# A list of jobs for the first pieces, rotary scalings spread over steps, and va's accumulators begun in pairs: one change to a two-layer encoder kernel on one core

## The chip, the core and the metric

The kernel runs on one core of a Trainium2 chip. The metric is the device time of one execution in microseconds (us), the median of several executions. A core has TensorE (PE, matrix multiplications; PEld is its loading of the stationary operand), VectorE (DVE), ScalarE (ACT), GpSimd (POOL), and SyncE (SP), which here only issues DMAs. Every engine works through its own instructions strictly in the order in which they were written down; what crosses engines is held together by semaphores.

## What is computed

Two groups of tokens, a prompt of 512 and a sample of 256, go through the same two layers. The reference, cut to what matters here:

```python
def _layer(x, c, norm_g, w_ada, b_ada, w_in, b_gate, rpb, q_norm_g, k_norm_g, w_pa, w_pb, w_out):
    ...
    mod = jax.nn.silu(c) @ w_ada + b_ada
    shift, scale, gate = jnp.split(mod, 3, axis=-1)
    hid = _rms_norm(x, norm_g) * (1.0 + scale[:, None, :]) + shift[:, None, :]
    proj = hid @ w_in
    ...
    qa, ka, va, za, qb, kb, vb, zb, ga, gb = jnp.split(proj, split_at, axis=-1)
    ...
    ya = (oa * jax.nn.silu(za)) @ w_pa
    qh = _axial_rope(_rms_norm(qb.reshape(b, n, GQA_Q_HEADS, HEAD_DIM), q_norm_g))
    kh = _axial_rope(_rms_norm(kb.reshape(b, n, GQA_KV_HEADS, HEAD_DIM), k_norm_g))
    ob = _gqa_attention(qh, kh, vb.reshape(b, n, GQA_KV_HEADS, HEAD_DIM))
    yb = (ob * jax.nn.silu(zb)) @ w_pb
    ...
    merged = g_a * ya + g_b * yb
    return x + gate[:, None, :] * (merged @ w_out)
```

Here `oa` is neighbourhood attention over qa, ka and va, and `g_a`, `g_b` are sigmoids of ga and gb.

After two layers a last RMSNorm gives y. Every large product is made of three matmuls, since each operand is split into a high part (rounded) and a low part (what the rounding left): high by high, high by low, low by high.

## The kernel before

Features lie on the partitions, 8 blocks of 128 (`KC`). `hid[g, k]` is the pair `hh`, `hl` (high and low part of `hid`) of block k for group g, 0 for the prompt and 1 for the sample. Weights come in units of 128 x 1024 (`raw`, 512 KB a DMA, two buffers); `split_one` (L220) makes `whi` on ACT and `low` makes `wlo` on DVE, four buffers each.

**Steps.** Most of the kernel is a row of steps: `step(fn)` (L162) writes down one step's matmuls, then everything that `defer(k, fn)` (L151) put k steps later, then pieces of attention from `slots`. So the code's order is every engine's order, and "deferred by two" means that an evacuation stands behind the matmuls of the next steps in the order of writing.

**The first pieces** (L1043 to L1204) are not steps. `put(t, fn)` notes a piece with a due time t, worked out by hand from constants in `SC` (`T0`, `U`, `ML`, `RL`, `FL`, `HL`, `PL`, `WL`, `TS`, `TR`), and the pieces are then written down in order of t. They are:

- loads in the order x (8 blocks), then four times 8 pieces of `w_ada` (`adaraw`, 256 KB each) and one unit of va's weights, then the sample's x (`x0s`) and the masks;
- for each quarter i and each of scale (`sec` 1) and shift (`sec` 0), two products `q_mul` on PE (tile `adap`), then `c_rows` on ACT, `c_col` on PE (tile `adat`), `c_fin` on DVE; so 16 of `q_mul` and 8 of `c_col`;
- the sum of squares of x: `square` on ACT, adds on POOL and DVE, `sq_sum` on PE (`ssps`), then 1/sqrt by Newton's steps on DVE (`ms`, `ny`, `na`) and its spread to all partitions on PE (`rb`); for the sample later the same;
- per block k: `hid_t` on DVE, `hid_hi` on ACT, `hid_lo` on DVE;
- the 16 pieces of va's prompt part (`va_prompt`, L639: for each k the token tiles 0, 1 and then 2, 3, six matmuls `accw` a piece);
- `warm`: matmuls on a tile of zeros (`junk`) that compute nothing, 10 at the start and one each 0.45 of the due time up to 17.

After them come `va_sample` (8 steps), the four pairs of branch A's q and k, then qb, kvb, za and the rest.

**va's accumulators.** `va_prompt` takes all four accumulators at its first piece: tiles 0 to 2 from `ps_acc` (three PSUM buffers), tile 3 from `ps_o` (one buffer). In layer 1 the three `ps_acc` buffers have just held the output products of layer 0 (`accs`), which `wev` reads (L1578).

**The rotary part.** `q_evac` and `kv_evac` copy a product to `rr` and sum its squares; after `SC["QF"]` = 5 steps `rope_finish` (L1309) runs Newton's steps on DVE and at once multiplies every `rr` by the result, four tiles for the prompt's q, two for the sample's q, three for k. The transposes of q follow in `q_tr_p` (from `SC["QT"]` = 8 steps, every two steps) and `q_tr_s` (from `SC["QST"]` = 9), those of k in `ktr` (8 steps after kvb); their PSUM tiles are `qt` and `kt`, from `ps_t` with two buffers, and DVE and ACT read them into `GQ` and `GK`.

Of the kernel before, what the change touches and what calls it, by code (L numbers as in the profile page):

```python
# [7 lines left out]
F32 = mybir.dt.float32  # L8
# [8 lines left out]
KC = 8  # L17
# [7 lines left out]
SC = dict(  # L25

    LA=7,
    U=0.68,

    ML=0.25,  # L30
    RL=0.75,
    FL=0.6,
    HL=0.5,
    PL=0.3,
    WL=2.6,

    SG="PGPVPGPV",
    TS=1,
    TR=2.5,
    WARM=(10, 1, 17.0, 0.45),  # L40

    PW=("wor01", "wor11", "va3"),

# [2 lines left out]
    RQ=31,  # L46

    QF=5,
    QT=8,
    QTT=2,  # L50
    QS=6,
    QST=9,
    KF=6,
    KT=8,
    SGQ=12,
# [14 lines left out]
def trunk(ctx: ExitStack, tc: tile.TileContext, xT, wst, wad, wsd, vec, gain, trig, mask, eye, rpb, yT):  # L70
# [568 lines left out]
    def va_prompt(l):  # L639

        accs = {}
        v4s.clear()

        def piece(k, h):
            need_unit(("va", l), k // 2)
            if not accs:
                for i in range(4):
                    accs[i] = (ps_acc.tile([128, NP], F32, tag="acc", name="accw") if i < 3
                               else ps_o.tile([128, NP], F32, tag="o", name="accw"))
            for i in (2 * h, 2 * h + 1):  # L650
# [368 lines left out]
    with tc.manual_schedule():  # L1019
# [20 lines left out]
            V.tensor_scalar(out=bhalf[:, 8 * l:8 * l + 8], in0=v_bada(l, 2), scalar1=0.5, scalar2=None, op0=ALU.mult)  # L1040
        V.tensor_scalar(out=bgh, in0=vecs[:, 80:112], scalar1=0.5, scalar2=None, op0=ALU.mult)

        plan = []  # L1043

        def put(t, fn):
            plan.append((t, len(plan), fn))
# [17 lines left out]

        def q_load(sec, k):
            raw = galloc([128, 2, 256], F32, "adaraw")
            S.dma_start(out=raw, in_=wad[sec, k])
            quarter[sec, k] = raw
# [17 lines left out]
        def c_rows(sec, i):  # L1086
            rows_of[sec, i] = ada_rows(acc_of.pop((sec, i)))

        def c_col(sec, i):
            rows_of[sec, i] = ada_col(rows_of[sec, i])  # L1090

        def c_fin(sec, i):
            ada_fin(0, sec, i, rows_of.pop((sec, i)))

        def q_plan(sec, i):
# [20 lines left out]

        def square(k):
            sq[k] = galloc([128, NP], F32, "sq")
            A.activation(out=sq[k], in_=xs[0][k], func=AF.Square)

        def sq_add(k, base, eng):
            eng.tensor_add(out=sq[base], in0=sq[base], in1=sq[k])
            gfree(sq.pop(k))

        def sq_sum(k, first, last):
            if first:
                hcell["ps"] = ps_t.tile([128, 4], F32, tag="t", name="ssps")
            for i in range(4):
                mm(hcell["ps"][:, i:i + 1], sq[k][:, 128 * i:128 * i + 128], ones[:, 0:1],
                   first and i == 0, last and i == 3)  # L1130
            gfree(sq.pop(k))

        def sample_square(k):
            q = galloc([128, NS], F32, "sq")
            A.activation(out=q, in_=xs[1][k], func=AF.Square)
            sq[k] = q

        def sample_add(k):
            if k == 0:
                ssq[1] = sq.pop(0)  # L1140
            else:
                G.tensor_add(out=ssq[1], in0=ssq[1], in1=sq[k])
                gfree(sq.pop(k))

        for k in range(KC):
            kind = SC["SG"][k]
            put(tx[k], lambda k=k: square(k))
            if kind in "VG":
                put(tx[k] + 0.6, lambda k=k, kind=kind: sq_add(k, k - 1, G if kind == "G" else V))
                sq_of = k - 1  # L1150
            else:
                sq_of = k
            if k == KC - 1 or SC["SG"][k + 1] == "P":
                first = sq_of == 0
                t = tx[k] + SC["TS"] + (1.2 if sq_of != k else 0.6)
                put(t, lambda k=sq_of, first=first, last=k == KC - 1: sq_sum(k, first, last))
        tr_ = max(tx[-1] + SC["TR"], t - 0.4)
        for i, sl in enumerate(rms_chain(0, hcell)[1:]):
            put(tr_ + (0.5, 2.7)[i], sl[0])
        tr_ += 3.2  # L1160
        for i in range(4):
            put(tu[i], lambda: split_one(False))
            put(tu[i] + 1.0, low_all)
        va_steps = va_prompt(0)
        th_ = tr_
        tp = 0
        for k in range(KC):
            th_ = max(th_ + 0.7, ta[1, k // 2])
            put(th_, lambda k=k: hid_t(0, 0, k, xs[0][k], hcell["rb"], hst, True))
            t = max(th_ + 0.7, ta[0, k // 2] + 0.6 * (k % 2))  # L1170
            put(t, lambda k=k: hid_hi(0, 0, k, hst))
            put(t + SC["HL"], lambda k=k: hid_lo(0, 0, k, hst))
            tp = max(tp + 2.7, t + SC["HL"] + 0.6 + SC["PL"], tu[k // 2] + SC["WL"])
            for h in range(2):
                put(tp + 1.35 * h, lambda k=k, h=h: step(va_steps[2 * k + h]))


        scell, sst = {}, {}
        for k in range(KC):
            put(txs[k] + 0.1, lambda k=k: sample_square(k))  # L1180
            put(txs[k] + 0.6, lambda k=k: sample_add(k))
        t = txs[-1] + 2.0
        for i, sl in enumerate(rms_chain(1, scell)):
            put(t + (0, 0.4, 2.0)[i], sl[0])
        t += 2.6
        for k in range(KC):
            put(t, lambda k=k: hid_t(0, 1, k, xs[1][k], scell["rb"], sst, True))
            put(t + 0.45, lambda k=k: hid_hi(0, 1, k, sst))
            put(t + 0.9, lambda k=k: hid_lo(0, 1, k, sst))
            t += 0.85  # L1190
        W0, W1, WE, WS = SC["WARM"]
# [6 lines left out]
        put(-100, lambda: warm(W0))  # L1198
        t = T0
        while t < WE:  # L1200
            put(t, lambda: warm(W1))
            t += WS
        for _, _, fn in sorted(plan, key=lambda p: p[:2]):
            fn()  # L1204
        xd = None
        for l in range(DEPTH):

# [101 lines left out]
            def rope_finish(rs, ss):  # L1309

                n, nh = ss.shape[1], ss.shape[2]
                V.tensor_scalar(out=ss, in0=ss, scalar1=1.0 / 64, scalar2=EPS, op0=ALU.mult, op1=ALU.add)
                y = newton(ss.rearrange("p t h -> p (t h)"), n * nh).rearrange("p (t h) -> p t h", h=nh)
                t = 0
                for r in rs:
                    k = r.shape[1]
                    V.tensor_mul(out=r, in0=r, in1=y[:, t:t + k, :].unsqueeze(3).to_broadcast([128, k, nh, 64]))
# [489 lines left out]
```

## Time and profile before

| what | us |
|---|---|
| median of 3 executions | 1269.31 (1268.28 to 1269.43) |
| the profiled execution | 1263.48 |
| its span, first to last instruction | 1261.5 |
| PE busy | 1222.2 |
| DVE busy | 810.8 |
| ACT busy | 580.8 |
| POOL busy | 362.3 |

Times in the trace count from the start of the span. "Busy" on PE counts a matmul as busy while it is in the array, also at the slower clock; a row of the windows view gives that clock as PEclk (1.00 is full speed). In a row of the timeline stand the start, the duration, the engine, line and operation with its tiles and shapes, the count of merged instructions, and in brackets the engine's idle time before it with what ended it. A row of the waits view has the total, the times and the longest.

### The profile page before, as it was taken

Reading aid. Unit: us, or ns where it says so; the run is one execution under the profiler, and the core shown is the slowest. Engines: PE = TensorE matmul, PEld = TensorE weight load, DVE = VectorE, ACT = ScalarE, POOL = GpSimd, SP = SyncE. Lnnn points to the kernel's source line nnn. Section 1 sums busy time; section 2 is a strip of 40 time slices with the busy share of each in tenths; the row PEclk is TensorE's granted clock in tenths of the full one; section 3 lists DMA queues with packets and bytes.
Section 4 is the critical chain, followed back from the end, with each engine's and each line's share of the span. In section 5 each row is a group of like instructions: output and inputs, shape, how many; then the busy total and the mean of one; then the engine's idle time right before and its main releaser. Section 6 shows DMA issues by size and latency. Waiting matters only on the chain.

```text
span 1261.5 us, 19544 instructions
## 1 busy us (share of the span) xinstructions
PE 1222.2 (97%) x7301; PEld 1067.4 (85%) x7301; DVE 810.8 (64%) x1600; ACT 580.8 (46%) x1229; POOL 362.3 (29%) x391
## 2 busy tenths in 40 slices
PE   9899999899999999999989999979999999999997
PEld 6589988888989988887888998878989988878887
DVE  3467876785555457999375678778655545683435
ACT  3347764555555432323153676545555543232323
POOL 0214444443222131111041353644422221221102
PEclk9999998899999999999999999999999999999998
DMA  9333231110111125555452333211111012332334
GB/s 354 126 106 89 81 98 35 36 66 18 51 50 51 44 74 159 177 172 182 147 171 80 93 92 89 59 43 50 35 51 49 19 47 87 125 110 68 112 105 150
DMA packets 48845, 118.28 MB, mean 94 GB/s; under 512 B 5488, under 2 KB 13040, under 8 KB 48752
## 3 DMA queue, kind: packets, MB, share of 16 engines
q1 hardware_dynamic: 48608, 116.98, 29.7%
q8 instruction: 57, 0.93, 0.3%
q14 instruction: 36, 0.29, 0.1%
q10 hardware_dynamic: 144, 0.07, 0.0%
HBM read 110.74 MB, written 6.29 MB: 93 GB/s over the span
## 4 chain that ended last, share of the span: by engine, by line
PE 75%; DVE 14%; ACT 5%; issue 3%; POOL 2%; DMA 0%; DVEq 0%; ACTq 0%; POOLq 0%
PE accp L124 33%; PE accs L124 16%; PE accw L124 8%; PE go L124 3%; PE gtp L944 3%; DVE adaacc L454 3%; PE gsp L124 3%; DVE wlo L237 3%; PE acct L124 2%; ACT p L782 1%; PE sp L124 1%; PE junk L124 1%; PE op L124 1%; DVE ptl L711 1%; ACT whi L231 1%
## 5 line engine op out<-in xcount | busy, mean ns | idle before, releaser
L124 PE MATMUL accp<-hh,whi 128*128 128x512 f32 x512 | 203.0, 396 | 0.0
L124 PE MATMUL accp<-hh,wlo 128*128 128x512 f32 x512 | 200.2, 391 | 2.1 <-DVE wlo L237 2.1
L124 PE MATMUL accp<-hl,whi 128*128 128x512 f32 x512 | 200.1, 391 | 0.0
L237 DVE TENSOR_TENSOR wlo<-raw,whi 128x1024 fp32r<-128x1024 f32 x119 | 157.7, 1326 | 14.9 <-ACT whi L231 14.2
L933 POOL TENSOR_TENSOR gp<-gp,gss 128x512 f32<-128x512 f32 x80 | 89.3, 1118 | 205.8 <-DVE gss L931 179.6
L124 PE MATMUL accs<-hh,whi 128*128 128x256 f32 x512 | 145.9, 285 | 0.0
L124 PE MATMUL accs<-hh,wlo 128*128 128x256 f32 x512 | 144.8, 283 | 0.0
L124 PE MATMUL accs<-hl,whi 128*128 128x256 f32 x512 | 144.7, 283 | 0.0
L231 ACT ACTIVATE whi<-raw 128x1024 fp32r<-128x1024 f32 x124 | 129.9, 1053 | 16.6 <-PE accw L124 8.2
L124 PEld LDWEIGHTS accp<-hh,wlo 128*128 128x128 f32 x512 | 96.1, 188 | 24.4 <-DVE wlo L237 3.8
L124 PEld LDWEIGHTS accp<-hh,whi 128*128 128x128 f32 x512 | 96.3, 188 | 17.6
L124 PEld LDWEIGHTS accp<-hl,whi 128*128 128x128 f32 x512 | 96.4, 188 | 17.4
L124 PEld LDWEIGHTS accs<-hl,whi 128*128 128x128 f32 x512 | 97.9, 191 | 1.4
L124 PEld LDWEIGHTS accs<-hh,whi 128*128 128x128 f32 x512 | 97.8, 191 | 1.3
L124 PEld LDWEIGHTS accs<-hh,wlo 128*128 128x128 f32 x512 | 97.8, 191 | 0.0
L1519 POOL TENSOR_TENSOR th<-th 128x512 f32<-128x512 f32 (+1 forms) x32 | 43.4, 1367 | 171.2 <-DVE th L1512 170.7
L706 ACT ACTIVATE pth<-gtp 128x512 fp32r<-128x512 f32 x80 | 47.8, 597 | 93.0 <-PE go L124 73.3
L454 DVE SCALAR_TENSOR_TENSOR adaacc<-adaraw,csil,adaacc 128x512 f32<-128x512 f32 x112 | 86.6, 828 | 3.9 <-DMA adaraw<-in_wsd 3.9
L711 DVE TENSOR_TENSOR ptl<-gtp,pth 128x512 fp32r<-128x512 f32 x80 | 54.6, 685 | 47.3 <-ACT pth L706 47.3
L124 PE MATMUL accw<-whi,hh 128*128 128x512 f32 x192 | 79.2, 413 | 4.8 <-ACT hh L292 3.0
L124 PE MATMUL accw<-whi,hl 128*128 128x512 f32 x192 | 77.0, 401 | 1.1 <-DVE hl L298 1.1
L124 PE MATMUL accw<-wlo,hh 128*128 128x512 f32 x192 | 76.7, 399 | 0.0
(246 smaller groups left out, 2961.4 us busy)
## 6 DMA issues: line engine op xcount, KB each, us to landing
raw<-in_wst SPq DMA_DIRECT2D x124, 512.0 KB, 3.6
adaraw<-in_wsd SPq DMA_DIRECT2D x64, 256.0 KB, 3.2
adaraw<-in_wad SPq DMA_DIRECT2D x32, 256.0 KB, 6.0
u<-in_rpb SPq DMA_DIRECT2D x16, 354.5 KB, 5.0
u<-in_rpb SPq DMA_DIRECT2D x16, 236.5 KB, 4.3
out_y<-y SPq DMA_DIRECT2D x12, 256.0 KB, 2.5
x<-in_xT SPq DMA_DIRECT2D x8, 256.0 KB, 4.6
res<-in_xT SPq DMA_DIRECT2D x8, 256.0 KB, 3.3
```

Of the source, the lines that this page charges most:

```text
L124: T.matmul(out=out, lhsT=lhsT, rhs=rhs, start=start, stop=stop, skip_group_check=True)
L231: A.activation(out=hi, in_=r, func=AF.Copy)
L237: eng.tensor_sub(out=lo, in0=r, in1=hi.bitcast(F32))
L454: V.scalar_tensor_tensor(out=acc[n, h, g], in0=r, scalar=c, in1=acc[n, h, g], op0=ALU.mult, op1=ALU.add)
L706: A.activation(out=h, in_=t, func=AF.Copy)
L711: V.tensor_sub(out=lo, in0=t, in1=h.bitcast(F32))
L782: A.activation(out=P[:, j, :], in_=P[:, j, :], func=AF.Exp, scale=-1.0, bias=ss[:, j:j + 1], accum_out=ss[:, 2 + j:3 + j])
L933: G.tensor_mul(out=pv_, in0=pv_, in1=ss[:, 4:4 + n].unsqueeze(2).to_broadcast([128, n, w]))
L944: T.transpose(t[:, q, 128 * j:128 * j + 128], src, ident)
L1519: G.tensor_add(out=t[:, sl], in0=t[:, sl], in1=mrg[k][:, sl])
```

## The change

Four things change. The first pieces become jobs: `job(eng, dur, deps, fn, rank, at)` names the engine, a guessed duration, the jobs it depends on and an earliest time, and `run_jobs` takes again and again the job that can start first, with `rank` deciding between equals; loads and `warm` stay at due times. `warm` falls to one each 0.8 up to 16. The sample's x is loaded ahead of the fourth unit of va's weights, the prompt's `ssps` moves from `ps_t` to `ps_acc`. In `va_prompt` each accumulator is taken when it is first written, tile 0 is the one in `ps_o`, and in layer 1 the second and third piece change places. In `rope_finish` only the first two tiles are scaled at once; the third and fourth are deferred by one step. The transposes of q move from 8 to 9 (prompt) and from 9 to 12 steps (sample).

```diff
-    WARM=(10, 1, 17.0, 0.45),
+    WARM=(10, 16.0, 0.8),
...
-    QT=8,
+    QT=9,
...
-    QST=9,
+    QST=12,
...
         def piece(k, h):
             need_unit(("va", l), k // 2)
-            if not accs:
-                for i in range(4):
-                    accs[i] = (ps_acc.tile([128, NP], F32, tag="acc", name="accw") if i < 3
+            for i in (2 * h, 2 * h + 1):
+                if k == 0:
+                    accs[i] = (ps_acc.tile([128, NP], F32, tag="acc", name="accw") if i
                                else ps_o.tile([128, NP], F32, tag="o", name="accw"))
...
-        return [lambda k=k, h=h: piece(k, h) for k in range(KC) for h in range(2)]
+        seq = [(k, h) for k in range(KC) for h in range(2)]
+        if l:
+            seq[1:3] = seq[2:0:-1]
+        return [lambda k=k, h=h: piece(k, h) for k, h in seq]
...
+        def run_jobs(lag=0.12):
+            done, t_free, queue = {}, dict(PE=0.0, ACT=0.0, DVE=0.0, POOL=0.0), list(jobs)
+            out = []
+            while queue:
+                best = None
+                for j in queue:
+                    if any(d not in done for d in j["deps"]):
+                        continue
+                    ready = max([j["at"]] + [done[d] + lag for d in j["deps"]])
+                    start = max(ready, t_free.get(j["eng"], 0.0))
+                    key = (start, j["rank"], j["n"])
+                    if best is None or key < best[0]:
+                        best = key, j
...
         def q_plan(sec, i):
+            deps = [jrow[sec, i - 1]] if i else []
             for k in range(4 * i, 4 * i + 4):
-                t = load(1, lambda k=k: q_load(sec, k)) + SC["ML"]
+                t = load(1, lambda k=k: q_load(sec, k))
                 if k % 2:
-                    put(t, lambda k=k: q_mul(sec, k))
-            t += SC["RL"]
-            put(t, lambda: c_rows(sec, i))
-            put(t + 0.4, lambda: c_col(sec, i))
-            put(t + 0.4 + SC["FL"], lambda: c_fin(sec, i))
+                    m = job("PE", 0.6, deps, lambda k=k: q_mul(sec, k), 0, t)
+                    deps = [m]
+            jrow[sec, i] = job("ACT", 0.4, [m], lambda: c_rows(sec, i), 0)
+            c = job("PE", 0.5, [jrow[sec, i]] + last_fin, lambda: c_col(sec, i), 0)
+            jfin[sec, i] = job("DVE", 0.4, [c], lambda: c_fin(sec, i), 0)
...
+        for k in range(KC):
+            t = job("DVE", 0.74, [jrb, jfin[1, k // 2]], lambda k=k: hid_t(0, 0, k, xs[0][k], hcell["rb"], hst, True), 1 + k)
+            h = job("ACT", 0.71, [t, jfin[0, k // 2]], lambda k=k: hid_hi(0, 0, k, hst), 1 + k)
+            lo = job("DVE", 0.8, [h], lambda k=k: hid_lo(0, 0, k, hst), 1 + k)
+            for h in range(2):
+                jva.append(job("PE", 1.42, [lo, jlo[k // 2]] + jva[-1:] + ([jsum[-1]] if not k else []),
+                               lambda n=2 * k + h: step(va_steps[n]), 2 + k, 16.0))
...
-                for r in rs:
+                for i, r in enumerate(rs):
                     k = r.shape[1]
-                    V.tensor_mul(out=r, in0=r, in1=y[:, t:t + k, :].unsqueeze(3).to_broadcast([128, k, nh, 64]))
+
+                    def scale(r=r, k=k, t=t):
+                        V.tensor_mul(out=r, in0=r, in1=y[:, t:t + k, :].unsqueeze(3).to_broadcast([128, k, nh, 64]))
+
                     t += k
+                    if i < 2:
+                        scale()
+                    else:
+                        defer(i // 2, scale)
```

The first place is the start on PE, the last rows ahead of va's first matmul (`accw`). Before:

```order
L124 MATMUL rb<-ident,ny 128x128 x4
L124 MATMUL junk<-cst 128x512
L124 MATMUL adap<-adaraw,c_104 32x256 x4
L124 MATMUL junk<-cst 128x512 x3
L124 MATMUL adat<-sel,rows 128x2 x2
L124 MATMUL junk<-cst 128x512 x3
L124 MATMUL adap<-adaraw,c_104 32x256 x4
L124 MATMUL accw<-whi,hh_327 128x512
```

And now, the same place:

```order
L116 MATMUL adap<-adaraw,c_104 32x256 x4
L116 MATMUL rb<-ident,ny 128x128 x4
L116 MATMUL junk<-cst 128x512
L116 MATMUL adat<-sel,rows 128x2 x2
L116 MATMUL adap<-adaraw,c_104 32x256 x8
L116 MATMUL accw<-whi,hh_316 128x512
```

Ahead of va's first matmul stood 41 of `junk` and five of `q_mul` (a `q_mul` is `adap` x4); now 23 of `junk` and six of `q_mul`, the last two of them right ahead of it.

The second place is DVE in the rotary part of layer 0, at the end of Newton's steps for the prompt's q: `rr` are the scalings, `ptl` the low part of a transposed probability tile for which PE waits, `GQ` the reading of a `qt`. Before:

```order
L374 SCALAR_TENSOR_TENSOR ny<-na,ny 128x32
L1317 TENSOR_TENSOR rr<-rr,ny 128x512 x4
L711 TENSOR_TENSOR ptl<-tp,pth 128x512
L1294 TENSOR_REDUCE qss<-rsq 128x8
L675 SCALAR_TENSOR_TENSOR GQ<-qt,GQ 64x512 x2
L1294 TENSOR_REDUCE qss<-rsq 128x8
```

And now:

```order
L366 SCALAR_TENSOR_TENSOR ny<-na,ny 128x32
L1339 TENSOR_TENSOR rr<-rr,ny 128x512 x2
L705 TENSOR_TENSOR ptl<-tp,pth 128x512
L1339 TENSOR_TENSOR rr<-rr,ny 128x512 x2
L1314 TENSOR_REDUCE qss<-rsq 128x8 x2
```

`ptl` moved ahead of two of the four scalings, and the first `GQ` behind both sums of squares.

The third place is DVE some 40 us later, where k's scalings end and `kt` is read into `GK`. Before:

```order
L1317 TENSOR_TENSOR rr<-rr,ny 128x256 x3
L1420 SCALAR_TENSOR_TENSOR zt<-zt,accp 128x512
L237 TENSOR_TENSOR wlo<-raw,whi 128x1024
L686 TENSOR_TENSOR GK<-kt,GK 64x512
L687 TENSOR_TENSOR GK<-kt,GK 64x512
```

And now:

```order
L1339 TENSOR_TENSOR rr<-rr,ny 128x256 x2
L1447 SCALAR_TENSOR_TENSOR zt<-zt,accp 128x512
L229 TENSOR_TENSOR wlo<-raw,whi 128x1024
L1339 TENSOR_TENSOR rr<-rr,ny 128x256
L680 TENSOR_TENSOR GK<-kt,GK 64x512
```

The third scaling of k, on which the sample's part of `kt` rests, now stands behind za's `zt` and a `wlo`.

More of the change, by code (lines that the diff above doesn't have):

```diff
@@ L1041, in trunk, with job @@
         V.tensor_scalar(out=bgh, in0=vecs[:, 80:112], scalar1=0.5, scalar2=None, op0=ALU.mult)
+        jobs = []
+        def job(eng, dur, deps, fn, rank=0.0, at=0.0):
+            jobs.append(dict(eng=eng, dur=dur, deps=list(deps), fn=fn, rank=rank, at=at, n=len(jobs)))
+            return len(jobs) - 1
+        def run_jobs(lag=0.12):
[11 more added lines that the diff above has]
+                        best = key, j
+                (start, _, _), j = best
+                done[j["n"]] = start + j["dur"]
+                if j["eng"] in t_free:
+                    t_free[j["eng"]] = start + j["dur"]
+                out.append((start, j["n"], j["fn"]))
+                queue.remove(j)
+            for _, _, fn in sorted(out + plan, key=lambda p: p[:2]):
+                fn()
         plan = []
-        def put(t, fn):
-            plan.append((t, len(plan), fn))
         def load_x(g, k):
@@ L1114, in trunk, with square @@
-        put(T0 + U * dma[0], lambda: S.dma_start(out=masks, in_=mask))
+        load(1, lambda: S.dma_start(out=masks, in_=mask))
+        hcell, hst = {}, {}
         sq = {}
[L1117 to L1123, printed above, removed]
+        def square(g, k):
+            sq[g, k] = galloc([128, RNG[g][1]], F32, "sq")
+            A.activation(out=sq[g, k], in_=xs[g][k], func=AF.Square)
@@ L1125, in sq_sum, with sq_add @@
+        def sq_add(g, k, base, eng):
+            eng.tensor_add(out=sq[g, base], in0=sq[g, base], in1=sq[g, k])
+            gfree(sq.pop((g, k)))
         def sq_sum(k, first, last):
             if first:
[L1127 removed]
+                hcell["ps"] = ps_acc.tile([128, 4], F32, tag="acc", name="ssps")
             for i in range(4):
[L1129 removed]
+                mm(hcell["ps"][:, i:i + 1], sq[0, k][:, 128 * i:128 * i + 128], ones[:, 0:1],
@@ L1157, in trunk @@
[L1157 to L1175, printed above, removed]
@@ L1178, in trunk @@
[L1178 to L1190, printed above, removed]
@@ L1191, in trunk @@
-        W0, W1, WE, WS = SC["WARM"]
+            gfree(sq.pop((0, k)))
+        jsum = []
+        for k in range(KC):
+            j = job("ACT", 0.63, [], lambda k=k: square(0, k), 1, tx[k])
+            kind = SC["SG"][k]
+            if kind in "VG":
+                eng, dur = (G, 1.1) if kind == "G" else (V, 0.8)
+                j = job("POOL" if kind == "G" else "DVE", dur, [jprev, j], lambda k=k, eng=eng: sq_add(0, k, k - 1, eng), 1)
+            jprev, base = j, k - (kind in "VG")
+            if k == KC - 1 or SC["SG"][k + 1] == "P":
+                jsum.append(job("PE", 0.95, [j] + jsum[-1:],
+                                lambda k=base, first=not jsum, last=k == KC - 1: sq_sum(k, first, last), 0))
@@ new lines, in trunk @@
+        j = jsum[-1]
+        for (fn,), (eng, dur) in zip(rms_chain(0, hcell)[1:], (("DVE", 2.4), ("PE", 1.0))):
+            j = job(eng, dur, [j], fn, 0)
+        jrb = j
+        jlo = {}
+        for i in range(4):
+            h = job("ACT", 1.05, [], lambda: split_one(False), 1.5 + 2 * i, tu[i])
+            jlo[i] = job("DVE", 1.33, [h], low_all, 1.5 + 2 * i)
+        va_steps = va_prompt(0)
+        jva = []
+        for k in range(KC):
+            t = job("DVE", 0.74, [jrb, jfin[1, k // 2]], lambda k=k: hid_t(0, 0, k, xs[0][k], hcell["rb"], hst, True), 1 + k)
[4 more added lines that the diff above has]
+                               lambda n=2 * k + h: step(va_steps[n]), 2 + k, 16.0))
@@ new lines, in trunk, with sample_sum @@
+        scell, sst = {}, {}
+        jadd = []
+        for k in range(KC):
+            j = job("ACT", 0.36, [], lambda k=k: square(1, k), 12, txs[k])
+            if k:
+                jadd = [job("POOL", 0.6, [j] + jadd, lambda k=k: sq_add(1, k, 0, G), 12)]
+            else:
+                jadd = [j]
+        def sample_sum():
+            ssq[1] = sq.pop((1, 0))
+            sums[0][0]()
+        sums = rms_chain(1, scell)
+        j = job("PE", 0.4, jadd + [jfin[0, 3], jfin[1, 3]], sample_sum, 0)
```

68 lines of the change are left out of this document (22 added, 46 removed).

## The prediction

> **What bounds the kernel now.** I read the page first, then PE's waits, then the clock, then the timeline at the three places that the change touches.
>
> ```profile
> PE 1222.2 (97%) x7301; PEld 1067.4 (85%) x7301; DVE 810.8 (64%) x1600; ACT 580.8 (46%) x1229; POOL 362.3 (29%) x391
> ```
>
> PE is busy for 1222.2 of 1261.5 us, no other engine for more than 64%. So time is to be had only where PE waits, where it runs at the slower clock, or where it does work that computes nothing. PE's waits over the whole span, the two longest groups (total, times, longest):
>
> ```profile
> PE qt L1356 <- DVE rr L1317: 7.8, 2, 3.9
> PE op L124 <- DVE ptl L711: 7.5, 4, 2.8
> ```
>
> Both belong to the rotary part: the transposes of the sample's q wait 3.9 us in each layer for their scalings, and a product of branch A's attention waits up to 2.8 for `ptl`, which stands behind four scalings on DVE. A wait costs twice. These rows of the windows view have the stretch, PE's busy time and, third from the end, PEclk:
>
> ```profile
> 54.90:58.20 3.30, 3.10 (x7) 2.48 (x8) 1.28 (x2) 1.06 (x4) 3.06 (x4) 0.50 0.73 233
> 211.90:218.70 6.80, 6.02 (x28) 6.02 (x29) 1.32 (x3) 0.28 (x1) 3.97 (x4) 0.50 0.01 2
> 235.80:242.60 6.80, 5.23 (x24) 4.97 (x25) 5.39 (x13) 1.78 (x5) 1.54 (x3) 0.50 0.02 6
> 655.60:659.00 3.40, 3.40 (x10) 2.62 (x9) 2.55 (x3) 1.98 (x3) 1.49 (x2) 0.50 0.35 97
> 846.80:850.10 3.30, 3.18 (x15) 2.92 (x15) 2.77 (x6) 1.04 (x4) 0.00 (x0) 0.50 0.02 5
> ```
>
> Each stands right behind a wait, and half of PE's busy time in it is lost: 1.6 to 1.7 us for a short one, 3.0 and 2.6 for the long ones. The wait of 1.8 us quoted below was enough for the one at 655.6.
>
> **The start.** The first row is va's matmuls up to 80 us, with the first and last start; then PE's waits from 22 to 77 us; then its timeline.
>
> ```profile
> L124 PE MATMUL accw<-whi,hh x48: 389/397/628, 22.5 to 75.5; 128*128 128x512 f32 x48
> ```
>
> ```profile
> PE accw L124 <- ACT hh L292: 3.0, 4, 1.1
> PE accw L124 <- DVE hl L298: 1.1, 4, 0.6
> PE ssps L124 <- POOL sq L1142: 0.9, 1, 0.9
> ```
>
> ```profile
> 26.59 0.50 PE L124 MATMUL adat<-sel,rows 128*128 128x2 f32 x4
> 27.02 0.64 PE L124 MATMUL adap<-adaraw,c 128*32 128x256 f32 x8
> ...
> 65.05 0.50 PE L124 MATMUL accw<-whi,hh 128*128 128x512 f32 x1 [1.11 <-ACT hh L292]
> ...
> 76.22 0.39 PE L124 MATMUL accp<-hh,whi 128*128 128x512 f32 x1
> ```
>
> From 22.5 to 76.2 are 53.7 us. The work in them: 24 steps of va at 1.40 (the last eight run undisturbed from 65.05 to 76.22), 33.5; 11 `q_mul` at 0.6, 6.6; 6 `adat` at 0.43, 2.6; the sample's `ssps` and `rb`, about 1.1. That is 43.8. Of the other 9.9, 5.0 are the waits above, 1.6 the half clock at 54.9, and 3.3 I can't name singly (changes between kinds of matmuls, operands that come a little late).
>
> When can va start now? By the order, behind the sixth `q_mul`, whose second load is the fourth of the second eight. From SP's timeline, and the DMA view for 10 to 35 us (KB each, median from issue to landing):
>
> ```profile
> 11.47 5.72 SPq L1067 DMA_DIRECT2D adaraw<-in_wad  x8
> ```
>
> ```profile
> adaraw<-in_wad SPq DMA_DIRECT2D x25, 256.0 KB, 6.0
> ```
>
> The eight are issued 0.72 apart, so that load at 13.6; it lands at 19.6, and the product is done at 20.2. The other input: the first `raw` is issued one load ahead, at 10.8, and lands near 16.8; `whi` takes 1.05 and then:
>
> ```profile
> 21.46 1.23 DVE L237 TENSOR_TENSOR wlo<-raw,whi 128x1024 fp32r<-128x1024 f32 x1
> 22.60 0.75 DVE L298 SCALAR_TENSOR_TENSOR hl<-x,ada_shift,hh 128x512 fp32r<-128x512 f32 x1
> ```
>
> That gives 19.8. What has so far kept va until 22.5 is PE's own order: 41 matmuls of zeros, now 23. So va starts at 20.2; one `q_mul` less is left behind it. The waits on `hh` go: shift and scale of a quarter are now taken as soon as its loads are there, and those are issued ahead of va's demand, which PE alone sets. The sample's squares, which hold up `ssps`, are loaded earlier; their next wait I put at 0.3, and 0.5 at a `q_mul` that PE reaches before its load. Of the 3.3 I keep half. End of va: 20.2 + 43.2 + 0.8 + 1.6 = 65.8 instead of 76.2, **a gain of 10.4**. With all 3.3 kept it is 8.8, with none 12.0; 6 if the start also falls to the half clock. What follows (pairs of q and k) is shifted as a whole, since its loads hang on buffers that va's own steps free.
>
> **va in layer 1.** The view is PE's waits from 640 to 660 us.
>
> ```profile
> PE accw L124 <- DVE xn L1578: 1.8, 1, 1.8
> ```
>
> Tiles 2 and 3 waited for the last `accs` buffer. Now a piece that only reuses tiles 0 and 1 comes between, some 1.4 us, and the last buffer is needed only by the second half of the piece after it, 0.7 later: 2.1 cover 1.8. Tile 0's `ps_o` has no user here. **Gain 1.8 + 1.7** of half clock = 3.5; 1.8 if the clock would have held anyway.
>
> **The rotary part.** DVE, layer 0:
>
> ```profile
> 209.53 2.50 DVE L1317 TENSOR_TENSOR rr<-rr,ny 128x512 f32<-128x512 f32 x4
> 211.94 0.69 DVE L711 TENSOR_TENSOR ptl<-tp,pth 128x512 fp32r<-128x512 f32 x1
> 212.54 0.68 DVE L1294 TENSOR_REDUCE qss<-rsq 128x8 f32<-128x512 f32 x1
> 219.66 1.39 DVE L675 SCALAR_TENSOR_TENSOR GQ<-qt,GQ 64x512 fp32r<-64x512 f32 x2 [6.45 <-ACT GQ L674]
> ...
> 228.92 0.42 DVE L1382 TENSOR_TENSOR vg<-acct,vg 128x256 fp32r<-128x256 f32 x1 [0.45 <-ACT vg L1381]
> ...
> 254.72 1.10 DVE L1317 TENSOR_TENSOR rr<-rr,ny 128x256 f32<-128x256 f32 x3
> 255.85 0.69 DVE L1420 SCALAR_TENSOR_TENSOR zt<-zt,accp 128x512 f32<-128x512 f32 x1
> 256.46 1.22 DVE L237 TENSOR_TENSOR wlo<-raw,whi 128x1024 fp32r<-128x1024 f32 x1
> ```
>
> and PE:
>
> ```profile
> 225.18 0.60 PE L1343 MATMUL qt<-ident,rr 128*128 128x128 f32 x4
> ...
> 228.48 0.60 PE L1343 MATMUL qt<-ident,rr 128*128 128x128 f32 x4
> ...
> 243.54 0.48 PE L124 MATMUL accp<-hh,whi 128*128 128x512 f32 x1
> ...
> 255.29 1.08 PE L1396 MATMUL kt<-ident,rr 128*128 128x128 f32 x6 [0.60 <-DVE rr L1317]
> ```
>
> `ptl` now stands behind two scalings, 1.25 us earlier, so PE goes on at 211.4; its wait is 1.6. The qt wait of 3.9 goes: three steps later are over 4 us. But PE then runs into the next thing that DVE owes, the scalings of k in front of `kt`, and here lies most of what I take off the gain.
>
> PE's way there: the rest of `op`, `tp` and `os`, 1.5; a kvb step is (228.48 - 225.18 - 0.36) / 2 = 1.47 with 0.36 for a transpose; a za step (255.29 - 0.60 - 243.54) / 8 = 1.39. Five kvb steps and two `qt` end at 211.4 + 1.5 + 7.35 + 0.7 = 220.95; there the first `vg` is due. Seven more steps, four `qt` and eight of za: 10.3 + 1.4 + 11.1, PE is at `kt` at 243.75.
>
> DVE's way, from that `vg` to the last scaling of k, before:
>
> ```profile
> 228.00:255.80 27.80, 21.36 (x53) 0.88 0.13 38
> ```
>
> 21.4 us of work (the row has DVE's busy time only) in 27.8, the rest waits for PE. Into the same stretch the change puts one more `GQ` (1.4), and, ahead of the third scaling, `zt` and `wlo` (0.7, 1.2); the three waits of `vg` on ACT stay (0.45 each, 1.4). Sum 26.1. `vg` comes 0.9 behind 220.95 (three short ACT copies), so DVE is through at 247.9 and `kt` done at 248.3, against 256.2 before: 7.9 gained, with a new wait of about 4 in front of `kt`. In layer 1 the waits are the same, but the half clock took only 3.2 busy us there instead of 11.3 (rows above), so 4.0 less is to be gained: 3.9. The new wait is longer than that of 655.6, so I charge it a short stretch at half clock, 1.7 a layer. **Rotary part: 7.9 + 3.9 - 3.4 = 8.4.** Its bounds: 20 without the wait at `kt`, 1.6 if `op` still costs its clock and `kt` two stretches.
>
> A rule of the Trainium skill speaks against these clock prices. TensorE: Matmul & The Clock Gate, Part 1: The HAM clock gate, lets PE fall to half clock after an idle window of about 3.4 us, and warns only of gaps above about 3 us. The rows at 655.6 disagree: 1.8 us of wait was enough. By the rule the sum would keep the 3.4 that I charge at `kt`.
>
> **The sum.** 10.4 + 3.5 + 8.4 = 22.3. The profiled execution took 1263.5 (span 1261.5), which makes it 1241.2 (1239.2). The median of the runs shown is 1269.3, 5.8 above the profiled one; I take the same difference off: **1247.0 us**.
>
> **Rivals.**
> - *No wait at `kt`.* POOL's slow stretches on DVE may be shorter and Newton's steps with them; for it speaks that DVE idled 6.45 us in one place. Against it, the 26.1 against PE's 22.8. Gain 2 x (4.2 + 1.7) = 12 more: 1235.
> - *The wait at `kt` eats the rotary gain.* The row at 211.9 shows that the half clock can last 6.8: two stretches in each layer, and `op`'s 1.6 falling into one window, cost 6.8 more: 1254.
> - *A cold start.* 18 matmuls of zeros fewer leave PE less busy from 7 to 20 us. If it drops to half clock there, va starts some 2 later and its first windows run slow: gain 6 instead of 10.4, 1251.
> - *The page's rule holds*: `kt` costs no clock, 1243.6. The Trainium skill's section named above would give this; the traces here are against it.
> - *Slower than before.* The half clock that 54.9 shows behind 1.6 us of waits could persist from the start through va, with short waits on loads keeping each window under the mark. The 43.2 us of work would take 86, va would end near 109, 33 later than now, and less the other 11.9 the change would be slower by 21: 1290. It turns the sign once over 45 us of PE's work run at half clock. Against it: from 20 on PE has under 1 us of idle time by my count, and every half-clock row above ended after 3.4 to 6.8.
>
> **How the numbers follow.** Forecast 0.50; no wait at `kt` 0.13; the wait eats it 0.14; cold start 0.12; page's rule 0.04; several of the losses together, within 0.2% of before, 0.03; slower 0.04. 0.2% is about what a measurement of this kernel tells from no change. So faster 0.93, same 0.03, slower 0.04. The range must take in 1235 and 1254 with the bounds of the start: 1234 to 1257, and leaves out the last two cases and a little of the tails.
>
> **What would show it.** First `accw` near 20 and first `accp` near 66; no wait on `xn` in layer 1; no wait of `qt` on `rr`, `op`'s near 1.6; and before `kt` a wait of some 4 us in each layer, in two parts, the second for the third scaling, with PEclk 0.50 behind it. If `kt` doesn't wait, my DVE sum is wrong; if va starts after 22, the start was not PE's order.

## The result, and the profile after

| runs of one chip | before, median (n) | this, median (n) | ratio, 95% interval |
|---|---|---|---|
| the change, first measurement | 1268.80 (4) | 1253.62 (4) | 0.9879 (0.9848 to 0.9910) |
| the change, once more (`whole`) | 1265.82 (11) | 1254.55 (6) | 0.9899 (0.9877 to 0.9922) |

The change is faster by 1.0 to 1.2%. Its profiled execution took 1254.29 us (span 1252.5), 9.2 less than that of before; 22.3 were forecast between the two.

The page's row of PE and its row of granted clocks in 40 slices:

```profile
PE 1216.3 (97%) x7283; PEld 1065.0 (85%) x7283; DVE 813.2 (65%) x1600; ACT 580.9 (46%) x1229; POOL 358.3 (29%) x391
...
PEclk6999999999999999999999999999999999999999
```

PE is still what bounds the kernel. The 6 at the left is new: one slice is 31 us, and the mean clock in the first is only 0.6 to 0.7. The same row of before:

```profile
PEclk9999998899999999999999999999999999999998
```

PE's waits after the change (total, times, longest):

```profile
PE kt L1423 <- DVE rr L1339: 10.7, 4, 2.9
PE op L116 <- DVE ptl L705: 5.2, 4, 1.6
PE rb L116 <- DVE ny L366: 3.1, 2, 1.7
PE ssps L116 <- POOL sq L1147: 2.9, 2, 1.9
```

Gone are `qt` behind `rr` (7.8), `accw` behind `hh` (3.0) and `accw` behind `xn` (1.8), and `op` has shrunk from 7.5 to 5.2. In their place stand `kt` behind `rr` (10.7 in two layers), `rb` behind `ny` in layer 1, and the sample's `ssps`. The stretches at half clock ahead of the last 5 us of the span, by the windows view (length, then busy time of PE, PEld, DVE, ACT and POOL, then PEclk, share of the DMA engines, GB/s):

```profile
8.31:28.79 20.48, 19.89 (x99) 12.70 (x97) 6.09 (x20) 5.16 (x9) 1.27 (x1) 0.50 0.99 371
52.68:56.10 3.42, 3.42 (x11) 2.74 (x11) 2.10 (x13) 0.00 (x0) 0.00 (x0) 0.50 0.01 2
247.24:254.07 6.83, 4.69 (x22) 4.72 (x23) 6.69 (x11) 4.27 (x9) 1.71 (x1) 0.50 0.24 77
854.82:858.22 3.40, 2.68 (x13) 2.71 (x14) 3.33 (x6) 2.21 (x6) 0.29 (x1) 0.50 0.49 154
```

The first is the surprise: 20.5 us at half clock in the start, where before had none until 54.9. PE's timeline there, first the first two rows of before:

```profile
1.19 7.11 PE L124 MATMUL junk<-cst 128*128 128x512 f32 x18 [1.19 <-DVE cst L1023]
8.14 0.95 PE L124 MATMUL ssps<-ones,sq 128*128 128x1 f32 x8
```

And after the change:

```profile
1.19 4.73 PE L116 MATMUL junk<-cst 128*128 128x512 f32 x12 [1.19 <-DVE cst L1017]
6.95 1.05 PE L116 MATMUL ssps<-ones,sq 128*128 128x1 f32 x8 [1.03 <-POOL sq L1147]
7.87 0.84 PE L116 MATMUL junk<-cst 128*128 128x512 f32 x2
9.30 1.87 PE L116 MATMUL ssps<-ones,sq 128*128 128x1 f32 x8 [0.59 <-DVE sq L1147]
...
28.86 0.50 PE L116 MATMUL accw<-whi,hh 128*128 128x512 f32 x1
...
52.34 0.73 PE L116 MATMUL ssps<-ones,sq 128*128 128x1 f32 x4 [1.88 <-POOL sq L1147]
...
75.44 0.39 PE L116 MATMUL accp<-hh,whi 128*128 128x512 f32 x1
```

Twelve matmuls of zeros are over at 5.9, PE waits for POOL, and from 8.3 on the work ahead of va takes up to twice its time: eight matmuls of one column (`ssps`) 1.70 to 1.87 instead of 0.95. va begins at 28.86 (22.47 before, 20.2 forecast) and ends at 75.44 (76.22 before, 65.8 forecast).

Where the time went, by the start of the same matmul in both profiled executions:

| PE's matmul | before | after | step of the difference | forecast |
|---|---|---|---|---|
| first `accp` (start) | 76.22 | 75.44 | -0.8 | -10.4 |
| first `gsp` behind `kt`, layer 0 (rotary) | 261.96 | 257.44 | -3.7 | -6.2 |
| the sample's `rb`, layer 1 (va) | 664.55 | 657.89 | -2.1 | -3.5 |
| first `gsp` behind `kt`, layer 1 (rotary) | 870.54 | 862.73 | -1.2 | -2.2 |
| end of the span | 1261.5 | 1252.5 | -1.2 | 0 |

### The profile page after: what moved, and what is told of

The parts are those of the page before. It is cut to its first block, busy times and chain, and to the rows that moved or that the text cites. A ratio compares the mean times of both kernels' runs of the same rounds, so it can differ in the third digit from the quotient of the medians.

```text
span 1252.5 us, 19508 instructions
## 1 busy us (share of the span) xinstructions
PE 1216.3 (97%) x7283; PEld 1065.0 (85%) x7283; DVE 813.2 (65%) x1600; ACT 580.9 (46%) x1229; POOL 358.3 (29%) x391
## 4 chain that ended last, share of the span: by engine, by line
PE 78%; DVE 12%; ACT 4%; issue 3%; DMA 1%; POOL 1%; SPq 0%; DVEq 0%; POOLq 0%; ACTq 0%
PE accp L116 35%; PE accs L116 17%; PE accw L116 8%; PE go L116 3%; PE gsp L116 3%; PE gtp L938 3%; PE acct L116 3%; DVE adaacc L446 3%; DVE wlo L229 2%; ACT p L776 1%; PE sp L116 1%; PE adap L116 1%; PE op L116 1%; DVE ptl L705 1%; ACT whi L223 1%
## 5 line engine op out<-in xcount | busy, mean ns | idle before, releaser
L927 POOL TENSOR_TENSOR gp<-gp,gss 128x512 f32<-128x512 f32 x80 | 86.6, 1083 | 213.3 <-DVE gss L925 175.4
L903 DVE TENSOR_REDUCE gss<-gsp 128x1 f32<-128x512 f32 x64 | 43.9, 687 | 51.4 <-PE gsp L116 51.1
```

Source lines behind the costliest of these rows:

```text
L903: V.tensor_reduce(out=ss[:, 0:1], in_=sp, axis=AX.X, op=ALU.max, negate=True)
L927: G.tensor_mul(out=pv_, in0=pv_, in1=ss[:, 4:4 + n].unsqueeze(2).to_broadcast([128, n, w]))
```

## Experiments

### The three parts, each alone on the kernel before

`p_start` has the list of jobs and the new WARM, `p_va` the new order of pieces and of accumulators, `p_rope` the later steps and spread scalings.

```diff
# p_start
-    WARM=(10, 1, 17.0, 0.45),
+    WARM=(10, 16.0, 0.8),
...
+        run_jobs()
...
# p_va
...
+        if l:
+            seq[1:3] = seq[2:0:-1]
# p_rope
-    QT=8,
+    QT=9,
...
-    QST=9,
+    QST=12,
...
+                        defer(i // 2, scale)
```

> The kernel before with the new start alone (list of jobs, 23 matmuls of zeros). Theory 1, the clock eats the start: as in the trace of the whole change, PE falls to half clock near 8 us and stays there until va begins, va's first matmul comes at 27 to 30 instead of 22.5 and the first accp at 74 to 77 instead of 76.2, so the time is 0 to 2 us below before. Theory 2, the profiled execution of the change was an unlucky one: va starts at 20 to 22, the first accp is at 65 to 69, and the time is 8 to 11 us below before.

> The kernel before with va's new order of pieces and of accumulators alone. Theory 1: the wait on xn of 1.8 us and the half clock behind it go (3.4 us), and the wait of rb on ny that the whole change shows there (1.7 us) comes in their place, because PE reaches rb before DVE's Newton steps are done: 1.5 to 2 us below before. Theory 2: the wait of rb belongs to where POOL stood in that execution, it does not come here, and the time is 3.5 us below before.

> The kernel before with the rotary part alone (later transposes of q, scalings spread over steps). Theory 1, the trace of the whole change holds here too: in each layer two waits before kt of 2.5 and 2.9 us, half clock behind them, and 4 us gained in layer 0, 1 in layer 1: 5 us below before. Theory 2, as forecast: waits of some 4 us in each layer and 8.4 us below before.

Before had a median of 1265.64 us in 19 runs:

| run | median | ratio, 95% interval |
|---|---|---|
| `p_start` | 1258.70 | 0.9936 (0.9913 to 0.9960) |
| `p_va` | 1262.62 | 0.9972 (0.9950 to 0.9994) |
| `p_rope` | 1261.19 | 0.9954 (0.9939 to 0.9969) |

The medians differ from before by 6.9, 3.0 and 4.5 us, 14.4 together: about what the whole gives (11.3 and 15.2). **The start** lies between its two theories. PE's timeline and the clock:

```profile
25.48 0.50 PE L116 MATMUL accw<-whi,hh 128*128 128x512 f32 x1
...
70.97 0.39 PE L116 MATMUL accp<-hh,whi 128*128 128x512 f32 x1
```

```profile
7.59:21.24 13.65, 13.65 (x62) 9.31 (x62) 3.34 (x14) 3.04 (x6) 1.27 (x1) 0.50 1.05 391
```

The cold start is there, but 13.65 us long instead of 20.48, and va is done 5.3 earlier than before. **va**: the mechanism is theory 1's; PE's waits from 640 to 670 us are this one row, with `xn` gone:

```profile
PE rb L124 <- DVE ny L374: 1.8, 1, 1.8
```

The time, 3.0 below before with an interval of 0.8 to 6.3, lies between the two theories and doesn't decide.

**The rotary part** is theory 1: 4.5 us, and the waits at `kt` and the half clock behind them are those of the whole change (in layer 1 it lasts 6.75 here, two windows, and 3.40 in the first profile of the whole change):

```profile
PE kt L1403 <- DVE rr L1319: 10.7, 4, 2.9
```

```profile
248.40:255.10 6.70, 3.80 (x19) 3.75 (x19) 6.60 (x10) 4.99 (x10) 2.11 (x1) 0.50 0.26 78
855.95:862.70 6.75, 5.34 (x25) 5.37 (x26) 6.58 (x11) 3.57 (x8) 0.98 (x1) 0.50 0.25 78
```

### What lets the clock fall in the start

```diff
# s_dense
-    WARM=(10, 16.0, 0.8),
+    WARM=(10, 17.0, 0.45),
# s_front
-    WARM=(10, 16.0, 0.8),
+    WARM=(18, 16.5, 0.55),
# s_zeros
-    WARM=(10, 16.0, 0.8),
+    WARM=(16, 17.0, 1.5),
...
             gfree(sq.pop((0, k)))
+            warm(4)
```

> The whole change, with matmuls of zeros every 0.45 us up to 17 us instead of every 0.8 up to 16 (36 in all instead of 23). Theory 1, the clock eats the start: with them PE keeps full clock from 8 to 28 us, va begins at 20 to 22 instead of 28.9, the first accp is at 66 to 69 instead of 75.4, and the time is 6 to 9 us below that of the change (about 1246 where the change has 1253.6). Theory 2, the chain of loads, row sums and products sets va's start: the clock stays at full, but va still begins after 26 and the time stays within 2 us of the change.

> The whole change, with 18 instead of 10 matmuls of zeros put first (by the order of the program 21 instead of 12 then stand ahead of the first sums of squares) and the later ones every 0.55 us up to 16.5. Theory 1, the window decides: half clock follows because the window of 3.4 us around the first sums of squares holds a wait on POOL and matmuls of one column, little of zeros; with the zeros ahead of the wait every window up to 28 us stays at full clock, va begins at 20 to 22.5, the first accp is at 66 to 69, and the time is 5 to 8 us below that of the change (1253.6). Theory 2, what the denser zeros of the run before this one suggest: they do not hold the clock in this order of work, half clock follows the first sums again, va begins at 28 or later, and the time is that of the change within 2 us.

In both, theory 1 missed. `s_dense` had 1253.82 us (0.9890, 0.9849 to 0.9931), `s_front` 1253.53 (0.9901, 0.9864 to 0.9939), no different from `whole` (0.9899). In `s_dense` the clock fell at 9.94:

```profile
9.94:27.00 17.06, 17.06 (x73) 10.58 (x73) 2.98 (x15) 2.28 (x4) 0.57 (x1) 0.50 1.05 390
```

Its va began at 30.1, later than with fewer zeros (28.9): two matmuls of zeros took 1.22 there at half clock, and 0.71 at full clock. So theory 1's cure failed; what theory 2 expected, a late va at full clock, was not seen either. In `s_front` half clock followed the first sums again and va began at 27.8, about as its theory 2 has it. The windows of `s_front` show what was wrong with the cure:

```profile
4.74:8.16 3.42, 3.42 (x19) 2.85 (x17) 0.64 (x1) 1.94 (x4) 1.29 (x1) 1.00 0.96 311
8.16:11.57 3.41, 3.15 (x22) 2.60 (x23) 0.54 (x2) 2.49 (x4) 1.29 (x1) 1.00 1.04 395
11.57:25.22 13.65, 13.65 (x63) 7.74 (x63) 2.49 (x15) 1.32 (x3) 0.00 (x0) 0.50 1.04 390
```

The zeros put first saved one window, but behind the next one the clock fell, though PE counts as busy for 3.15 of its 3.41 us. Its timeline shows with what:

```profile
8.56 0.71 PE L116 MATMUL junk<-cst 128*128 128x512 f32 x2
9.10 0.95 PE L116 MATMUL ssps<-ones,sq 128*128 128x1 f32 x8
9.91 0.93 PE L116 MATMUL junk<-cst 128*128 128x512 f32 x3
11.10 1.46 PE L116 MATMUL ssps<-ones,sq 128*128 128x1 f32 x8 [0.26 <-POOL sq L1147]
```

Five matmuls of zeros at some 0.235 us are 1.2 of 3.41; the rest is matmuls of one column. If those don't count, the window was busy for a third. That became the next theory (wide matmuls must fill over half of every window, wherever its start falls), and four zeros behind each sum its test:

> The whole change with 17 matmuls of zeros first and four more right behind each of the four sums of squares (40 in all, fewer spread ones). Theory 1, PE falls to half clock where a window of 3.41 us has it busy with wide matmuls for less than about half: every window from 5 to 28 us is now above half, whatever the phase, so none is at 0.50; va begins at 20 to 22.5, the first accp is at 67 to 70 (the sample's ssps still waits 1.9), and the time is 4 to 7 us below that of the whole change. Theory 2, zeros don't hold the clock here or cost as much as they save: the start is at half clock again, or va begins after 25, and the time is within 2 us of the whole change.

```profile
6.60:10.02 3.42, 3.42 (x23) 2.97 (x21) 0.69 (x1) 3.10 (x6) 1.27 (x2) 1.00 1.02 371
10.02:13.43 3.41, 3.41 (x24) 3.06 (x24) 0.69 (x1) 0.33 (x1) 0.35 (x1) 1.00 1.05 395
```

```profile
22.50 0.49 PE L116 MATMUL accw<-whi,hh 128*128 128x512 f32 x1
```

The clock held up to the sample's `ssps` at 46.6, va began at 22.50 and ended at 69.63, 5.2 before `whole` (74.78). The four executions of `s_zeros` have mean clocks of 0.988 to 0.991. The median was 1251.86 (0.9882, 0.9857 to 0.9906), only 2.7 below `whole` where theory 1 has 4 to 7, and the two intervals overlap; what is shown is the gain at va. The 5 us last until layer 1's first `gsp` (857.48 against 862.92); near the end `accs` waits 1.9 for a `wlo` of POOL, half clock follows, and 1.9 are left at the end of the span. That wait is between 0 and 1.5 in the other profiles; what sets it stays open.

### The sample's sum

```diff
-                jadd = [job("POOL", 0.6, [j] + jadd, lambda k=k: sq_add(1, k, 0, G), 12)]
+                jadd = [job("POOL", 1.2, [j] + jadd, lambda k=k: sq_add(1, k, 0, G), 12)]
```

> The whole change, with 1.2 us instead of 0.6 for each of POOL's additions of the sample's squares in the list of jobs, which puts the sample's ssps three steps of va later on PE. Theory 1: the wait of 1.9 us before that ssps and the half-clock window behind it, which every execution of the change shows near 52, both go, and the time is 2.5 to 4 us below that of the whole change. Theory 2: rb and the sample's hid are then late and va's end or the pairs behind it wait for them: within 1 us of the whole change.

Theory 1: 1251.08 us (0.9876, 0.9849 to 0.9904), 3.5 below `whole`, though the two intervals overlap; from 48 to 72 us PE doesn't wait and the clock is 1.00, and va ends at 70.76 instead of 74.78, 4.0 earlier. The list priced one addition at 0.6; POOL's timeline of the change has seven at 1.0 each, and `ssps` had been placed for the shorter ones:

```profile
45.31 6.98 POOL L1147 TENSOR_TENSOR sq<-sq 128x256 f32<-128x256 f32 x7 [34.11 <-DMA raw<-in_wst]
```

### The waits before kt

```diff
# k_junk
                     t = ps_t.tile([128, n], F32, tag="t", name="kt")
+                    for _ in range(18 + 4 * g):
+                        mm(t[:, 0:256], cst, cst.unsqueeze(1).to_broadcast([128, 2, 128]), True, True)
# k_nodefer
-                    if i < 2:
+                    if i < 2 or n > 4 and nh == 2:
                         scale()
# k_both9: as k_nodefer, and
-    KT=8,
+    KT=9,
```

> The whole change, with 18 and 22 matmuls of zeros of 256 columns put ahead of the two groups of transposes kt, in the same PSUM tile: PE computes zeros where it waited for the scalings of k, 2.1 and 2.6 us at full clock. Theory 1, half of the price of kt is the clock: the transposes still start when their scalings are done, but no half clock follows in either layer, and the time is 3.4 (layer 0) and 1.7 to 3.4 (layer 1), together 5 to 7 us, below that of the change. Theory 2, the clock does not see matmuls of zeros there, or the zeros delay the transposes: the half clock behind kt stays and the time is that of the change within 1.5 us.

> The whole change, but the three scalings of k issued together again, the third not put off by a step (that of q stays spread). Theory 1, the second wait of kt is the price of putting it off behind zt and wlo (0.7 and 1.2 us): it shrinks from 2.9 to under 0.5 in both layers, the first stays at 2.5, the half clock behind kt lasts one window of 3.4 at most, and the time is 5 to 9 us below that of the change. Theory 2: zt and wlo come 0.4 to 0.8 later and PE waits for one of them instead, so the time is within 2 us of the change.

> The whole change with the scalings of k together, and in addition the transposes kt one step of PE later. Theory 1: the first wait shrinks from 2.5 to about 1.1, the second stays under 0.5, no half clock follows in either layer, and the time is 10 to 13 us below that of the change. Theory 2: what hangs on kt (the evacuations of k to GK on DVE, about 4.4 us, and the first gsp) is then late: gsp waits for what kt no longer waits for, and the time is that of the kernel with the scalings together but kt where it was, within 2 us.

Before was at 1264.64 us there (6 runs).

| run | median | ratio, 95% interval |
|---|---|---|
| `k_junk` | 1248.96 | 0.9870 (0.9851 to 0.9888) |
| `k_nodefer` | 1244.66 | 0.9843 (0.9822 to 0.9865) |
| `k_both9` | 1248.03 | 0.9866 (0.9851 to 0.9882) |

`k_junk`, PE's timeline at `kt` and the windows behind it in both layers:

```profile
238.99 2.31 PE L116 MATMUL kt<-cst 128*128 128x256 f32 x18
241.54 0.67 PE L1425 MATMUL kt<-ident,rr 128*128 128x128 f32 x3 [0.25 <-DVE rr L1339]
```

```profile
239.00:251.00 12.00, 11.53 (x94) 10.99 (x93) 11.38 (x25) 5.00 (x10) 2.14 (x1) 1.00 0.15 51
844.80:856.80 12.00, 11.53 (x93) 10.95 (x93) 11.38 (x25) 5.00 (x10) 2.14 (x1) 1.00 0.15 50
```

The scalings come no sooner and the transposes wait as long as ever, only now behind zeros: and the clock stays at 1.00. Nothing is computed faster, yet the time is 5.6 below `whole` by the medians, 3.7 by the ratios (0.9870 against 0.9899). In the profiled executions the start's luck is in that too (first `accp` at 71.25 instead of 74.78); from the first `accp` to layer 0's first `gsp` it is 179.9 instead of 182.5. In layer 1, where half clock now follows `rb` instead, the same stretch from `rb` on is no shorter (205.2 and 205.0). So a part of the price of `kt` is the clock alone, as theory 1 has it. How much stays open: the profiles show 2.6 us in layer 0 and nothing in layer 1, and the intervals of the two ratios overlap; the 5 to 7 of theory 1 are not shown.

`k_nodefer` is theory 1 too, 9.9 below `whole` by the medians, 7.1 by the ratios. Its wait at `kt` is one of 2.5 in each layer; the second is gone:

```profile
PE kt L1423 <- DVE rr L1339: 4.9, 2, 2.5
```

`k_both9` shrinks the rest and gains nothing by it: its median is 3.4 above that of `k_nodefer`, more than the 2 of theory 2, though the intervals overlap. The mechanism is theory 2's. The wait has moved to `gsp`, which now stands closer behind `kt` than DVE can read `kt` into `GK`:

```profile
PE gsp L116 <- DVE GK L681: 3.3, 2, 1.7
...
PE kt L1423 <- DVE rr L1339: 2.1, 2, 1.1
PE gsp L116 <- ACT gp L913: 1.6, 2, 0.8
```

2.8 us less at `kt` in two layers, 4.9 more at `gsp`.

### The change again, and all cures together

> The whole change once more, unaltered, beside the kernels below on one chip. Theory 1, the spread between executions is the phase of the clock's windows: its executions have mean clocks from 0.984 to 0.991 and their times follow them, some 2.5 us for each 0.002 of clock, and the median is 11 to 15 us below before. Theory 2: the time doesn't follow the clock, and the first result (0.988 of before) is the change's true ratio within 0.001.

The six executions of `whole`, with the mean granted clock of each:

| clock | 0.982 | 0.983 | 0.984 | 0.984 | 0.986 | 0.988 |
|---|---|---|---|---|---|---|
| us | 1256.05 | 1254.82 | 1254.54 | 1254.56 | 1252.78 | 1249.51 |

Theory 1: 6.5 us over 0.006 of clock, 2.2 for each 0.002, where 0.002 of 1253 us are 2.5. Nearly the whole spread of this program goes with its time at half clock.

`x_best` is the change with the edits of `s_zeros`, `s_sample` and `k_nodefer`, and 18 zeros ahead of the first group of `kt` as in `k_junk`.

```diff
+                    for _ in range(18 if g == 0 else 0):
+                        mm(t[:, 0:256], cst, cst.unsqueeze(1).to_broadcast([128, 2, 128]), True, True)
```

> The whole change with four edits: zeros behind the sums of squares and the sample's ssps later, both as in the two runs above, the three scalings of k together, and 18 matmuls of zeros of 256 columns ahead of the first group of kt. Theory 1, the prices add up: 4 to 7 for the start, 2.5 to 4 for the sample, 9 for the scalings and 1.7 to 3.4 for the clock behind kt's first wait, together 17 to 23 us below the whole change, near 1233. Theory 2, what is saved at one place is lost at the next (a start that is earlier meets its loads, kt meets its scalings): less than 12 us below.

It took 1236.88 us (0.9769 of before, 0.9746 to 0.9793), 17.7 below `whole`, at the lower end of theory 1 and faster than both kernels. The page's row of clocks, and two of PE's timeline:

```profile
PEclk9999999999999999999999999999999999999999
```

```profile
21.91 0.50 PE L116 MATMUL accw<-whi,hh 128*128 128x512 f32 x1
...
65.33 0.39 PE L116 MATMUL accp<-hh,whi 128*128 128x512 f32 x1
```

Its mean clock is 0.998 against 0.984 for `whole`: no stretch at half clock but the last 5 us of the span.

## Why the prediction came out as it did

The time, 1253.6, is 6.6 above the forecast 1247.0 and inside the range; against its own basis, the profiled execution, the forecast is off by 13.1 (1254.3 against 1241.2). The two differ because of the 5.8 that I took from three runs of before: in the three later comparisons before's median lies 1.2 to 2.3 above its profiled execution. The two errors cancelled in part, so that the median came this close is partly luck. The gain was 15.2 and 11.3 us in the two comparisons, where 22.3 were forecast, and the time lies between two of the rivals, a cold start (1251) and the wait at `kt` that eats the rotary gain (1254); parts of both came true.

**The start, off by 9.6 of 10.4: a premise failed.** I wrote that the 41 matmuls of zeros had kept va until 22.5, and took their removal as pure gain. They had also held the clock, as `s_zeros` shows, where it stays at 1.00 with zeros put back beside the sums. Ahead of the first sum now stand 12 instead of 18; PE then waits for POOL, a window of 3.41 us has wide matmuls for less than half of it, and at half clock PE gets to va at 28.9 instead of 20.2. This was my rival "a cold start", with 0.12: its place and its mechanism were right, its chance too low; its price of 6 instead of 10.4 would do for `p_start` alone (6.9 in the runs), not for the whole change's profiled execution (0.8). The second failure is a number: I put the sample's next wait for its squares at 0.3; it was 1.88 with a window at half clock behind it. The two cures give 5.2 and 4.0 at va's end (`s_zeros`, `s_sample`), which is the 9.6 but for 0.4, and with both va ends at 65.33, near the 65.8 that I had worked out for a start without these two. That is luck in part: in `x_best` va begins at 21.9 and not at 20.2, and takes 43.4 us and not 45.6.

**va in layer 1, off by 1.4: one wait too few.** The wait on `xn` and its half clock went as described. But PE then reached the sample's `rb` 1.7 us before `ny` was done, since one step towards `ny` stood still on DVE (last section). I had followed PE only to the end of the wait that the change removes, not to the next thing that it waits for.

**The rotary part, off by 3.5 of 8.4: the mechanism right, two sizes wrong.** `qt` waits no more, `op` 1.6, and `kt` waits in two parts, the second for the third scaling behind `zt` and `wlo`: all as forecast. The two parts are 2.46 and 2.91 instead of together 4, since DVE took longer from the first `vg` to the last scaling:

```profile
220.82:249.23 28.41, 23.19 (x150) 20.48 (x148) 25.00 (x58) 14.49 (x30) 11.96 (x14) 0.97 0.18 53
```

28.4 us where I had 26.1. Its busy time, third behind the length, is 25.0 and I had 24.7; the rest is time between instructions, 3.4 where I had allowed 1.4 for waits of `vg`. Those waits are 2.0 (there are four, and one is 0.66); the other 1.4 lie between instructions that wait for nothing, some 0.8 of them between the short steps of Newton's iteration, which follow each other 0.21 apart with 0.17 of work:

```profile
242.88 0.17 DVE L359 TENSOR_SCALAR ny<-qss 128x12 int32<-128x12 int32 x1
243.09 0.17 DVE L361 TENSOR_SCALAR ny<-ny 128x12 int32<-128x12 int32 x1
```

That the busy times agree hides two differences. Newton's steps for k took 0.9 less than before; and the third scaling of k took 1.48, where all three together took 1.10 before and in `k_nodefer`. It started while POOL's `zt` ran, and ended 0.28 after it:

```profile
247.75 1.48 DVE L1339 TENSOR_TENSOR rr<-rr,ny 128x256 f32<-128x256 f32 x1
246.84 2.11 POOL L1450 TENSOR_TENSOR zt<-zt,oa 128x512 f32<-128x512 f32 x1 [4.02 <-DVE zt L1447]
```

So some 1.1 of the 2.91 is not the work ahead of this scaling but the scaling itself standing still; layer 1 has the same 1.48. I had counted it at its usual 0.4. That POOL's `zt` holds it up was not tested apart from the deferral.

And the clock: I charged one short window a layer, 1.7; layer 0 had two (6.83 us with PE busy for 4.69, so 2.3 lost), layer 1 one with 2.68. The second rival named this and I gave it 0.14. That the second part of the wait was the deferral's own price, `k_nodefer` shows.

**The clock by the page's rule** (rival of 0.04) fell. No wait at `kt` reached 3 us, and half clock followed in both layers; with zeros in the waits it did not. The Trainium skill, TensorE: Matmul & The Clock Gate, Part 1: The HAM clock gate, asks for a whole idle window of some 3.4 us, and the runs disagree: half a window is enough. The same part calls the window free-running and cold starts run-variable; here they agree, with clocks of 0.982 to 0.988 in six executions of one program.

**What I never weighed** is that the change hands time back to the clock as a whole. By the mean clock (time at half speed counted half), the profiled execution of before loses 0.013 x 1261.5 = 16.4 us and that of the change 0.016 x 1252.5 = 20.0.

## What to carry to other kernels

A matmul of zeros that computes nothing can be doing a job: before taking filler out, look at what share of each clock window PE is still busy with wide matmuls, and put it back beside the waits and the one-column matmuls, not spread evenly. A wait removed from an in-order engine is worth only what lies ahead of the next thing that this engine waits for, so follow it that far, with the pitch of short instructions and not their busy time. And an operation that is put off for one wait must not land behind work that nobody waits for yet: here `zt` and `wlo` ahead of k's third scaling, and POOL's work beside it, cost more than putting it off saved.

## What the hardware showed that was not expected

**The clock falls behind a window that lacks wide matmuls for half of it.** I took the windows of 3.41 us at full clock, up to 1215 us, in all 14 profiled executions, and added in each PE's idle time and that of its matmuls of one or two columns (up to 0.3 us each). With 0.9 to 1.75 us lost none of 129 was followed by half clock, with 1.95 or more all 43, in between 7 of 10. (Behind 1215 us, near the end, one with 1.96 was not, so the limit is not known to better than some 0.2 us.) In this count matmuls of zeros are busy and those of one column are not, and the starts show both: six of the windows followed by half clock had PE idle for only 0.26 to 1.15, and windows with nothing but zeros and one-column matmuls, as 6.60:10.02 of `s_zeros`, kept the clock. When PE regains full clock I could not tell: it took 13.65 us in one start and 20.48 in another.

**A short DVE instruction stood still for as long as POOL worked.** In the change's layer 1, on DVE and on POOL:

```profile
653.69 2.18 DVE L359 TENSOR_SCALAR ny<-ms 128x2 int32<-128x2 int32 x1
655.91 0.17 DVE L361 TENSOR_SCALAR ny<-ny 128x2 int32<-128x2 int32 x1
```

```profile
653.42 2.42 POOL L229 TENSOR_TENSOR wlo<-raw,whi 128x1024 fp32r<-128x1024 f32 x1 [2.27 <-ACT whi L223]
```

An operation on 128x2 takes 2.18 us, and ends when POOL's `wlo` ends (655.84). In before that `wlo` ran while DVE waited for PE's sum anyway. Without it `ny` would have come 2.0 earlier and the 1.7 us of `rb` would not be there; nine of the other profiles show it at the same place with 2.2 to 2.4 us. No run moved the `wlo` on purpose, but in `s_zeros` it came 0.02 us behind the start of this step, not ahead of it. There this step took 0.17, and the next one stood still, again until `wlo` ended (650.69):

```profile
648.45 2.26 DVE L361 TENSOR_SCALAR ny<-ny 128x2 int32<-128x2 int32 x1
648.27 2.42 POOL L229 TENSOR_TENSOR wlo<-raw,whi 128x1024 fp32r<-128x1024 f32 x1 [2.62 <-ACT whi L223]
```

So it is not the step but what POOL does at the time. The Trainium skill, SBUF — State Buffer, SBUF: two separate sides, says that DVE and GpSimd share a pair of ports as an exclusive lock; these rows agree.
